# A decoder block on one core: the weight sums of a seven-product up-projection, made by vector instructions or by accumulating DMA transfers

## The chip, the core and the metric

The kernel runs on one core of a Trainium2 chip. A core has a matrix engine (TensorE, PE in the profile; its weight loads are listed apart as PEld), a vector engine (VectorE, DVE), an activation engine (ScalarE, ACT), a general engine (GpSimd, POOL), and a sync engine (SyncE, SP), which here only issues transfers. Each takes its instructions in order from its own queue, and they wait for each other by semaphores. Sixteen DMA engines move data between DRAM and the on-chip buffer. The metric is the device time of one execution in microseconds (us), the median of several runs.

## The reference

One layer, float32, 2048 tokens of width 1024:

```python
h = rms_norm(x, attn_norm_w); proj = h @ w_in
y_ret = retention_group(...)      # 8 heads, chunkwise recurrent
y_mla = mla_group(...)            # 8 heads, causal softmax attention
x = x + concat(y_ret, y_mla) @ w_out
u = rms_norm(x, ffn_norm_w) @ w_up            # (1024, 5632): gate columns, then value columns
u = conv_b + sum(conv_w[j] * pad(u)[:, j:j+S] for j in range(3))
x = x + (silu(gate) * val) @ w_down           # gate, val: the halves of u, 2816 columns each
return rms_norm(x, final_norm_w)
```

The change concerns the product with `w_up` alone.

## The kernel before

The kernel has three parts. **Input projection** (`stage_1`): norm, latents, q, k and v, written to DRAM. **Retention beside attention**: two generators, `ret_stream` and `att_stream`, are drawn from in turn (`side_by_side`); attention goes through 32 groups (8 heads by 4 groups of 512 queries, `g` = 0 to 3, group `g` with 4g + 4 blocks of keys). For a group, q and k are loaded and split into a high and a low part (`split`: ACT writes the high part, POOL the low one, lines L65 and L69), the maxima are taken (`sm`), and for each block of keys PE makes scores `s`, ACT the exponential `pc`, POOL adds `pc` to the running sum `den` (L782), and PE multiplies by v (`o`). Retention loads 1 MB tiles `h<-hT_s` through SP (L530) and multiplies them by its weights (`pm`). **The feed-forward part**, in two halves of 1024 tokens: forms of the tokens (`half_0_forms`, `half_1_forms`), the up-projection with convolution and gate (`up`), the down-projection (`down`).

Every product is three matmuls on high and low parts (`mm3`, L73 to L75). The up-projection goes through 22 blocks `fb` of 128 gate and 128 value columns. In a block, the weights are a two by two matrix of pieces, gate and value by first and second half of the 1024 rows (`g0`, `g1`, `v0`, `v1`, 128x512 each), and the tokens are split in two likewise. Seven products instead of eight make the result (a scheme of Strassen's kind): PE multiplies seven sums of weight pieces with seven sums of token pieces, and DVE adds up the results in `u` (L1136).

- `token_forms` makes the seven token sums `F` once for each half.
- `weight_forms` makes the seven weight sums of each block: the plain pieces g0, v1, g1, and v0 + v1, v0 + v1 - g0, g0 - v0, g1 + g0 - v0 - v1. The four sums are POOL instructions (L1097 one addition, L1084 three subtractions), and each of the seven is split by ACT and POOL. It is a generator that runs ahead of the products: `LEAD` (9) forms before the first, then one form a product. The twelve places for split weights are `order`.
- `up_load` loads the four pieces of a block in two DMAs of 512 KB, a block ahead, into the four buffers `raws`.
- `conv` (L1141 to L1143) and the gate (L1166 to L1168) are ACT and DVE instructions of 1024 columns.

The order on each engine is not the order of the source: a scheduler in the compiler takes the instructions of all generators and puts on each engine those that it expects to be ready, by its own costs. An engine's queue is then fixed, and an instruction whose semaphore isn't there yet holds everything behind it. SP's transfers use eight semaphores in turn, so one also waits for the eighth before it. All SP transfers go through one queue of the DMA engines, in order.

Of the kernel before, what the change touches and what calls it, by code (L numbers as in the profile page):

```python
# [11 lines left out]
F32 = mybir.dt.float32  # L12
# [3 lines left out]
ALU = mybir.AluOpType  # L16
# [4 lines left out]
P = 128  # L21
# [3 lines left out]
KC = D // P  # L25
# [4 lines left out]
NFB = DFF // P  # L30
# [24 lines left out]
class Block:  # L55
# [500 lines left out]
    def att_stream(self):  # L556

        groups = [(h, g) for h in range(H) for g in range(4)]
        qs, done = {}, set()

        def maxima():
            for n, hg in enumerate(groups):
                while n > self.at + 2:
                    yield 0
                for c, qs[n] in self.att_max(*hg):
                    yield c
                done.add(n)
        self.at, mx, owed = 0, maxima(), 0.0
        for n, (h, g) in enumerate(groups):
            self.at = n  # L570
            while n not in done:
                yield next(mx)
            for c in self.att_group(h, g, qs.pop(n)):
                owed = min(owed + MAX_PACE, 2.0)
                while owed >= 1:
                    owed -= 1
                    c += next(mx, 0)
                yield c
        self.finish()
        yield 450  # L580

    def ret_chunk(self, p, ch, W, hs):
        nc, c1, c2, px = self.nc, self.r1, self.r2, self.pr_x
# [398 lines left out]
    def half_0_forms(self):  # L982

        nc, hn = self.nc, self.fs

        def rows(i):
            for j in range(2):
                nc.sync.dma_start(hn[2 * (i % 2) + j], self.hn_s[4 * j + i])
        for t in (8, 9):
            self.z0_load(t)  # L990
        rows(0)
        rows(1)
        for i in range(4):
            self.token_forms(i, hn[2 * (i % 2)], hn[2 * (i % 2) + 1])
            if i < 2:
                rows(i + 2)
            if i == 0:
                self.up_load(0)
            for t in (8 + 2 * i, 9 + 2 * i):
                m, y = self.ms[t % 2].rearrange("p (a k x) -> p a k x", a=2, k=4), self.ys[t % 2]  # L1000
                pss = [self.bank() for _ in range(2)]
                for kc in range(4):
                    self.out_mm(pss, m, kc, kc == 0, kc == 3)
                self.out_add(y, pss)
                nc.sync.dma_start(self.y_s[t], y)
                if t + 2 < NT:
                    self.z0_load(t + 2)
        self.up_start(0)
# [20 lines left out]
    def half_1_forms(self):  # L1029

        nc, hn, fnw = self.nc, self.fs, self.u2.rearrange("p a b -> p (a b)")
        for n in range(2):
            nc.sync.dma_start(self.ys[n], self.y_s[Z1_ORDER[n]])
        self.pay()
        for n, t in enumerate(Z1_ORDER):
            m, y = self.ms[n % 2].rearrange("p (a k x) -> p a k x", a=2, k=4), self.ys[n % 2]
            pss = [self.bank() for _ in range(2)]
            for kc in range(4, 8):
                self.out_mm(pss, m, kc, kc == 4, kc == 7)
            if n + 2 < TH:  # L1040
                self.z1_load(n + 2)
            self.out_add(y, pss)
            h, ss = hn[n % 4], self.cs.tile([P, 1], F32, name="ss")
            nc.scalar.activation(h, y, AF.Square, scale=D ** -0.5, accum_out=ss)
            nc.sync.dma_start(self.y_s[t], y)
            r = self.rstd(self.cs, ss, "n")
            nc.vector.scalar_tensor_tensor(h, y, r, fnw, op0=ALU.mult, op1=ALU.mult)
            if n + 2 < TH:
                nc.sync.dma_start(self.ys[n % 2], self.y_s[Z1_ORDER[n + 2]])
            if n == 1:  # L1050
                self.up_load(0)
            if n in (3, 5):
                self.token_forms(n // 2 - 1, hn[(n - 3) % 4], hn[(n - 2) % 4])
        self.up_start(1, 1)
        self.token_forms(2, hn[0], hn[1])
        for _ in range(3):
            next(self.prep)
        self.token_forms(3, hn[2], hn[3])

    def up_load(self, fb):  # L1060
        if fb < NFB:
            for j in range(2):
                self.nc.sync.dma_start(self.raws[(2 * fb + j + 2) % 4], self.a["w_up"][j * NFB + fb].rearrange("p k f -> p (k f)"))

    def up_start(self, half, lead=None):

# [12 lines left out]

    def weight_forms(self):  # L1080

        nc, a = self.nc, self.a
        t1, t2 = (self.fs[0][:, k * 512:(k + 1) * 512] for k in range(2))
        sub = lambda o, x, y: nc.gpsimd.tensor_tensor(o, x, y, op=ALU.subtract)  # L1084
        W = self.W = {}

        def raw(fb, j, k):
            return self.raws[(2 * fb + j + 2) % 4][:, k * 512:(k + 1) * 512]

        def put(fb, n, src):  # L1090
            W[fb, n] = self.slot_split(src, P)
        for fb in range(NFB):
            self.up_load(fb + 1)
            g0, g1, v0, v1 = (raw(fb, j, k) for j in range(2) for k in range(2))
            put(fb, 0, g0)
            yield
            nc.gpsimd.tensor_tensor(t1, v0, v1, op=ALU.add)  # L1097
            sub(t2, t1, g0)
            put(fb, 1, t2)
            yield  # L1100
            sub(v0, g0, v0)
            put(fb, 6, v0)
            yield
            put(fb, 4, t1)
            yield
            sub(g0, g1, t2)
            put(fb, 2, v1)
            yield
            put(fb, 3, g0)
            yield  # L1110
            put(fb, 5, g1)
            yield

    def up(self, half):

        nc, u, F, p1 = self.nc, self.u, self.F, self.p1
        ag, av = self.fs[2], self.fs[3]  # L1120
        u2, u3 = self.u2[:, 0], self.u2[:, 1]
# [5 lines left out]
        def product(fb, n):  # L1127
            ps = self.bank()
            wh, wl = self.W.pop((fb, n))
            for kc in range(4):  # L1130
                self.mm3(ps, wh[:, kc, :], wl[:, kc, :], F[:, n, 0, kc, :], F[:, n, 1, kc, :], kc == 0, kc == 3)
            next(prep, None)
            return ps

        def add(out, ps, x):
            nc.vector.tensor_tensor(out, ps, x, op=ALU.add)  # L1136

        def conv(acc, fb, j):
            w0, w1, w2, b = (self.cw[:, j * NFB + fb, k:k + 1] for k in range(4))
            x = u[:, j]  # L1140
            nc.scalar.activation(acc, x[:, 2:1026], AF.Identity, scale=w2, bias=b)  # L1141
            nc.vector.scalar_tensor_tensor(acc, x[:, 1:1025], w1, acc, op0=ALU.mult, op1=ALU.add)  # L1142
            nc.vector.scalar_tensor_tensor(acc, x[:, 0:1024], w0, acc, op0=ALU.mult, op1=ALU.add)  # L1143
        owed = None
        if half == 0:
            nc.vector.memset(u[:, :, 0:2], 0.0)
        for fb in range(NFB):
            nc.scalar.activation(p1, product(fb, 0), AF.Copy)
            add(u2, product(fb, 1), p1)
            add(u3, product(fb, 6), u2)  # L1150
            if owed:
                nc.sync.dma_start(*owed)
            ps = product(fb, 4)
            if half:
                nc.vector.tensor_copy(u[:, :, 0:2], self.tail[:, fb])
            add(u[:, 1, 514:], ps, u3)
            add(u2, ps, u2)
            add(u[:, 1, 2:514], product(fb, 2), u3)
            conv(av, fb, 1)
            add(u[:, 0, 514:], product(fb, 3), u2)  # L1160
            add(u[:, 0, 2:514], product(fb, 5), p1)
            conv(ag, fb, 0)
# [109 lines left out]
    def run(self):  # L1272
        tc, ctx = self.tc, self.ctx
        dp = ctx.enter_context(tc.tile_pool(name="scratch", bufs=1, space=DRAM))
# [7 lines left out]
        self.rden_s = dp.tile([4, H, 4, P], F32, name="rden_s")  # L1282
        self.y_s = dp.tile([NT, P, D], F32, name="y_s")
        self.hn_s = dp.tile([TH, P, D], F32, name="hn_s")
        self.g_s = dp.tile([2, NFB, P, HALF], F32, name="g_s")
        self.den_s = dp.tile([4, H, 4, P], F32, name="den_s")
        self.denl_s = dp.tile([4, H, 4, P], F32, name="denl_s")
# [53 lines left out]
def host_arrays(x, positions, attn_norm_w, w_in, ret_gn_w, mla_q_norm_w, w_uq, mla_kv_norm_w, w_ukv,  # L1341
# [8 lines left out]
    pe = uq[:, :, 64:]  # L1350
    pe_sw = np.concatenate([pe[:, :, 16:], pe[:, :, :16]], 2)
    ukv = g(w_ukv)[0].reshape(128, H, 128)
    w_up = g(w_up)[0].reshape(KC, P, 2 * NFB, P).transpose(2, 1, 0, 3)
    conv = np.concatenate([g(conv_w)[0], g(conv_b)], 0).reshape(4, 2 * NFB, P).transpose(2, 1, 0)
    arrays = dict(
        x=c(g(x)[0]),
# [46 lines left out]
```

## Time and profile before

| | |
|---|---|
| median of 3 runs | 2937.12 us (2935.92 to 2937.17) |
| profiled execution | 2932.35 us, its span 2930.5 us |
| granted clock of TensorE, mean | 0.976 |
| PE, DVE, ACT, POOL busy | 93%, 67%, 46%, 67% of the span |
| HBM read, written | 237.64 MB, 92.75 MB |

A row of the trace gives a start and a length in us from the span's start. In the groups of instructions a mean is in ns. An engine's idle time is put down to the engine that released it. A matmul row's length includes its way through the engine, so rows that follow each other overlap; the distance of starts (0.23 us for 512 columns) is the engine's pace.

### The profile page before, as it was taken

Reading aid. Unit: us, or ns where it says so; the run is one execution under the profiler, and the core shown is the slowest. Engines: PE = TensorE matmul, PEld = TensorE weight load, DVE = VectorE, ACT = ScalarE, POOL = GpSimd, SP = SyncE. Lnnn points to the kernel's source line nnn. Section 1 sums busy time; section 2 is a strip of 40 time slices with the busy share of each in tenths; the row PEclk is TensorE's granted clock in tenths of the full one; section 3 lists DMA queues with packets and bytes.
Section 4 is the critical chain, followed back from the end, with each engine's and each line's share of the span. In section 5 each row is a group of like instructions: output and inputs, shape, how many; then the busy total and the mean of one; then the engine's idle time right before and its main releaser. Section 6 shows DMA issues by size and latency. Waiting matters only on the chain.

```text
span 2930.5 us, 37500 instructions
## 1 busy us (share of the span) xinstructions
PE 2732.9 (93%) x12672; PEld 2217.2 (76%) x12672; DVE 1972.3 (67%) x3393; ACT 1347.0 (46%) x2544; POOL 1962.2 (67%) x1480
## 2 busy tenths in 40 slices
PE   7998999998999999988999999899985999999998
PEld 6976777776777777767887777688874888887887
DVE  8756776767676776744478888834276888887243
ACT  5435566666665566641433333334334443333343
POOL 2035566666656565653799999675658999995554
PEclk9999999999999999989999999999997999999999
DMA  7663121223212121346622221365562222224463
GB/s 258 226 207 91 45 77 61 69 68 97 67 56 66 44 66 59 94 116 203 233 79 72 80 86 67 101 232 169 165 204 69 87 74 78 87 72 170 144 198 107
DMA packets 153505, 332.85 MB, mean 114 GB/s; under 512 B 35032, under 2 KB 68568, under 8 KB 147168
## 3 DMA queue, kind: packets, MB, share of 16 engines
q1 hardware_dynamic: 153312, 330.45, 34.8%
q8 instruction: 100, 1.64, 0.2%
q14 instruction: 93, 0.76, 0.1%
HBM read 237.64 MB, written 92.75 MB: 113 GB/s over the span
## 4 chain that ended last, share of the span: by engine, by line
PE 42%; DVE 10%; issue 5%; ACT 3%; POOL 2%; DMA 2%; SPq 0%; ACTq 0%; DVEq 0%; POOLq 0%
PE b L75 12%; PE b L74 12%; PE b L73 12%; DVE w L1142 2%; ACT w L1141 2%; DVE u L1136 2%; DVE w L1143 1%; DVE w L1168 1%; DMA raw<-mixa_s 1%; DVE w L1167 1%; PE x L666 1%; ACT u L1166 1%; POOL w L69 1%; PE pm L75 1%; PE pm L74 1%
## 5 line engine op out<-in xcount | busy, mean ns | idle before, releaser
L69 POOL TENSOR_TENSOR w<-raw,w 128x512 fp32r<-128x512 f32 (+2 forms) x315 | 523.5, 1677 | 251.1 <-ACT w L65 239.3
L73 PE MATMUL b<-F,w 128*128 128x512 f32 x1232 | 488.8, 397 | 3.9 <-DVE u L1136 3.9
L75 PE MATMUL b<-F,w 128*128 128x512 f32 x1232 | 491.9, 399 | 0.0
L74 PE MATMUL b<-F,w 128*128 128x512 f32 x1232 | 487.5, 396 | 3.1 <-POOL F L69 3.1
L782 POOL TENSOR_TENSOR den<-den,pc 128x512 f32<-128x512 f32 (+2 forms) x256 | 294.5, 1150 | 231.4 <-ACT pc L771 212.8
L65 ACT ACTIVATE w<-raw 128x512 fp32r<-128x512 f32 (+2 forms) x328 | 214.4, 658 | 340.5 <-PE b L75 166.3
L73 PE MATMUL b<-w 128*128 128x512 f32 x832 | 329.9, 396 | 22.0 <-DVE u L1136 13.1
L75 PE MATMUL b<-w 128*128 128x512 f32 x832 | 328.2, 394 | 1.4 <-POOL w L69 1.2
L74 PE MATMUL b<-w 128*128 128x512 f32 x832 | 327.6, 394 | 0.0
L69 DVE TENSOR_TENSOR w<-xr,w 128x512 fp32r<-128x512 f32 x88 | 108.6, 1234 | 286.3 <-ACT w L65 286.3
L73 PEld LDWEIGHTS b<-F,w 128*128 128x128 f32 x1232 | 232.6, 189 | 65.8 <-DVE u L1136 11.1
L74 PEld LDWEIGHTS b<-F,w 128*128 128x128 f32 x1232 | 232.5, 189 | 61.8 <-POOL F L69 3.6
L75 PEld LDWEIGHTS b<-F,w 128*128 128x128 f32 x1232 | 232.5, 189 | 55.0
L1141 ACT ACTIVATE w<-u,cw 128x1024 f32<-128x1024 f32 x88 | 109.5, 1244 | 332.7 <-DVE u L1136 187.1
L773 DVE TENSOR_TENSOR pc<-s,pc 128x512 fp32r<-128x512 f32 (+1 forms) x320 | 197.3, 618 | 94.8 <-ACT s L772 78.1
L771 ACT ACTIVATE pc<-s 128x512 fp32r<-128x512 f32 (+1 forms) x320 | 173.0, 540 | 177.9 <-PE s L769 173.5
L1142 DVE SCALAR_TENSOR_TENSOR w<-u,cw,w 128x1024 f32<-128x1024 f32 x88 | 165.8, 1884 | 129.2 <-ACT w L1141 129.2
L73 PE MATMUL pm<-w,h 128*128 128x512 f32 x512 | 209.1, 408 | 12.2 <-DVE r_g L115 3.8
L69 POOL TENSOR_TENSOR w<-xr,w 128x512 fp32r<-128x512 f32 x110 | 205.5, 1881 | 9.4 <-ACT w L65 9.4
L74 PE MATMUL pm<-w,h 128*128 128x512 f32 x512 | 203.9, 398 | 0.0
L73 PEld LDWEIGHTS b<-w 128*128 128x128 f32 x832 | 158.6, 191 | 59.4 <-DVE u L1136 16.8
L75 PE MATMUL pm<-w,h 128*128 128x512 f32 x512 | 203.1, 397 | 0.0
(264 smaller groups left out, 6622.3 us busy)
## 6 DMA issues: line engine op xcount, KB each, us to landing
raw<-in_w_down SPq DMA_DIRECT2D x88, 512.0 KB
h<-hT_s SPq DMA_DIRECT2D x32, 1024.0 KB
xr<-in_w_up SPq DMA_DIRECT2D x44, 512.0 KB
raw<-in_w_up SPq DMA_DIRECT2D x44, 512.0 KB
g_s<-w SPq DMA_DIRECT2D x44, 512.0 KB
xr<-g_s SPq DMA_DIRECT2D x88, 256.0 KB
hT_s<-hT SPq DMA_DIRECT2D x16, 1024.0 KB
raw<-in_w_ret SPq DMA_DIRECT2D x16, 512.0 KB
```

Of the source, the lines that this page charges most:

```text
L65: nc.scalar.activation(hi, src, AF.Copy)
L69: eng.tensor_tensor(lo, src, f32(hi), op=ALU.subtract)
L73: mm(out, lhsT=lh, rhs=rh, start=start, stop=False)
L74: mm(out, lhsT=lh, rhs=rl, start=False, stop=False)
L75: mm(out, lhsT=ll, rhs=rh, start=False, stop=stop)
L666: mm(ps[:, x * P:x * P + 256], lhsT=l, rhs=r, start=n == 0, stop=n == len(ops) - 1)
L771: nc.scalar.activation(pc[:, 0, r0:], ps[:, r0:], AF.Exp, scale=ATT_SCALE)
L773: nc.vector.tensor_tensor(pc[:, 1, r0:], ps[:, r0:], f32(pc[:, 0, r0:]), op=ALU.subtract)
L782: nc.gpsimd.tensor_tensor(den[:, r0:], den[:, r0:], hi[:, r0:], op=ALU.add)
L1136: nc.vector.tensor_tensor(out, ps, x, op=ALU.add)
L1141: nc.scalar.activation(acc, x[:, 2:1026], AF.Identity, scale=w2, bias=b)
L1142: nc.vector.scalar_tensor_tensor(acc, x[:, 1:1025], w1, acc, op0=ALU.mult, op1=ALU.add)
```

## The change

The host lays out `w_up` so that g0, g1, v0 and v1 are four arrays of [22, 128, 512]. A new generator `sums`, drawn from once at the start of each attention group, makes four sums in DRAM (`sum_s`, 4 x 22 x 128 x 512 float32): s1 = v0 + v1, s2 = v0 + v1 + g0, s3 = v0 + g0, s4 = v0 + v1 + g0 + g1. Each is a copy from DRAM to DRAM issued by SP and one accumulating transfer issued by POOL (`accum_op=ALU.add`) that adds a second array to it. It does so for blocks 0 to 10 and then for 11 to 21: eight copies and eight accumulating transfers, each of 11 x 128 x 512 x 4 bytes = 2.88 MB. The gate pieces thereby have the opposite sign in s2 to s4; `up` turns two additions into subtractions the other way round, and one more in the gate's result. `weight_forms` has no additions left: it splits each of the seven pieces as it comes from DRAM, with a load of 256 KB for each of them (`form_load`), eight forms ahead, in half buffers of `raws`.

```diff
-        self.at, mx, owed = 0, maxima(), 0.0
+        self.at, mx, owed, sums = 0, maxima(), 0.0, self.sums()
         for n, (h, g) in enumerate(groups):
             self.at = n
+            next(sums, None)
...
+    def sums(self):
+        sy, po = self.nc.sync.dma_start, self.nc.gpsimd.dma_start
+        rows = lambda t: t.rearrange("b p f -> (b p f)").rearrange("(n x) -> n x", x=2048)
+        for part in range(2):
+            sl = slice(part * NFB // 2, (part + 1) * NFB // 2)
+            g0, g1, v0, v1 = (rows(self.a["w_up"][i][sl]) for i in range(4))
+            s1, s2, s3, s4 = (rows(self.sum_s[i][sl]) for i in range(4))
+            def more(t, x):
+                po(t, x, accum_op=ALU.add, max_dma_last_dim=2048)
+            yield sy(s1, v0)
+            yield sy(s3, v0)
+            yield more(s1, v1)
+            yield more(s3, g0)
+            yield sy(s2, s1)
+            yield
+            yield more(s2, g0)
+            yield
+            yield sy(s4, s2)
+            yield
+            yield more(s4, g1)
+            yield
...
+    def form_load(self, i):
+        if i < 7 * NFB:
+            fb, n = divmod(i, 7)
+            src = [self.a["w_up"][0], self.sum_s[1], self.sum_s[2], self.sum_s[0], self.a["w_up"][3], self.sum_s[3], self.a["w_up"][1]][n]
+            self.nc.sync.dma_start(self.form_raw(i), src[fb])
+    def form_raw(self, i):
+        return self.raws[(i // 2 + 2) % 4][:, (i % 2) * 512:(i % 2 + 1) * 512]
...
     def weight_forms(self):
-        for fb in range(NFB):
-            self.up_load(fb + 1)
-            g0, g1, v0, v1 = (raw(fb, j, k) for j in range(2) for k in range(2))
-            put(fb, 0, g0)
-            yield
-            nc.gpsimd.tensor_tensor(t1, v0, v1, op=ALU.add)
-            sub(t2, t1, g0)
-            put(fb, 1, t2)
-            yield
-            sub(v0, g0, v0)
-            put(fb, 6, v0)
...
-            sub(g0, g1, t2)
...
+        for i in range(4, 8):
+            self.form_load(i)
+        for i in range(7 * NFB):
+            fb, n = divmod(i, 7)
+            W[fb, (0, 1, 6, 4, 2, 3, 5)[n]] = self.slot_split(self.form_raw(i), P)
+            self.form_load(i + 8)
             yield
...
-            add(u2, product(fb, 1), p1)
-            add(u3, product(fb, 6), u2)
+            sub(u2, product(fb, 1), p1)
+            sub(u3, u2, product(fb, 6))
...
-            add(u[:, 0, 514:], product(fb, 3), u2)
+            sub(u[:, 0, 514:], product(fb, 3), u2)
```

Of SP's queue before, at the start of attention (q, k and v of the first group, and the next tiles `h` of retention):

```order
L462 DMA mqk<-in_mask_att 128x128 [waits DMAHW1_49,DVE_49,Pool_49]
L723 DMA raw<-q_s 96x512 [waits DMAHW2_49,Activation_49]
L530 DMA h<-hT_s 128x2048 [waits DMAHW3_49,PE_49]
L707 DMA raw<-k_s 64x512 [waits DMAHW4_49,DMAHW0_49,Activation_49]
L708 DMA raw<-kpe_s 34x512 [waits DMAHW5_49]
L710 DMA raw<-v_s 128x4x64 [waits DMAHW6_49]
L723 DMA raw<-q_s 96x512 [waits DMAHW7_49,DMAHW2_49,Pool_49]
L530 DMA h<-hT_s 128x2048 [waits PE_49]
```

The same place of SP's queue now (`sum_s` is the DRAM array of the sums):

```order
L462 DMA mqk<-in_mask_att 128x128 [waits DMAHW1_49,DVE_49,Pool_49]
L594 DMA sum_s<-in_w_up 64x11264 [waits DMAHW2_49]
L748 DMA raw<-q_s 96x512 [waits DMAHW3_49,Activation_49]
L732 DMA raw<-k_s 64x512 [waits DMAHW4_49,DMAHW0_49,Activation_49]
L733 DMA raw<-kpe_s 34x512 [waits DMAHW5_49]
L735 DMA raw<-v_s 128x4x64 [waits DMAHW6_49]
L595 DMA sum_s<-in_w_up 64x11264 [waits DMAHW7_49]
L748 DMA raw<-q_s 96x512 [waits DMAHW3_49,Pool_49]
L732 DMA raw<-k_s 64x512 [waits DMAHW5_49,DMAHW4_49,DMAHW6_49,DMAHW1_49,Pool_49]
L733 DMA raw<-kpe_s 34x512 [waits DMAHW2_49]
L735 DMA raw<-v_s 128x4x64
L530 DMA h<-hT_s 128x2048 [waits PE_49]
```

Two copies, and the loads of two groups, now stand ahead of the first tile `h`, which stood right behind the first load of q.

SP's queue now, 38 rows after the first copy: the last four of the eight copies (DMASW is a semaphore of an accumulating transfer).

```order
L602 DMA sum_s<-sum_s 64x11264 [waits DMAHW0_49,DMASW2_49]
L821 DMA den_s<-otl 1x512 [waits DMAHW1_49,Activation_49]
L595 DMA sum_s<-in_w_up 64x11264 [waits DMAHW2_49]
L748 DMA raw<-q_s 96x512 [waits DMAHW6_49,DMAHW5_49,DMAHW7_49,DMAHW3_49,Pool_49]
L598 DMA sum_s<-sum_s 64x11264 [waits DMAHW4_49,DMASW3_49]
L602 DMA sum_s<-sum_s 64x11264 [waits DMASW6_49]
L724 DMA mix_s<-m 128x2x128 [waits Activation_49]
L530 DMA h<-hT_s 128x2048 [waits PE_49]
L732 DMA raw<-k_s 64x512 [waits DMAHW0_49,Pool_49]
```

All sixteen transfers have been put into the first three attention groups, not one into each of 24 groups; three of these copies wait for accumulating transfers, the last for the seventh of the eight.

POOL's queue now, at the end of the third attention group (`den`: the running sum of the softmax; `pc`, `ot`: the group's end):

```order
L593 DMA sum_s<-in_w_up 1408x512 [waits DMAHW4_49]
L807 TENSOR_TENSOR den<-den,pc 128x512 [waits Activation_49,Pool_49] x2
L641 TENSOR_TENSOR vs<-vg,gam 128x128 [waits Activation_49]
L807 TENSOR_TENSOR den<-den,pc 128x384 [waits Activation_49,Pool_49]
L807 TENSOR_TENSOR den<-den,pc 128x256 [waits Activation_49,Pool_49]
L593 DMA sum_s<-in_w_up 1408x512 [waits DMAHW5_49]
L807 TENSOR_TENSOR den<-den,pc 128x256 [waits Activation_49,Pool_49]
L69 TENSOR_TENSOR q<-raw,q 96x512 [waits PE_49,Activation_49]
L69 TENSOR_TENSOR pc<-den,pc 128x512 [waits DVE_49,Activation_49]
L845 TENSOR_TENSOR ot<-ot,otl 64x512 [waits Activation_49]
```

These are the seventh and the eighth accumulating transfer; the eighth waits for the last copy, and the group's last addition to `den` stands behind it.

## Rows read from the trace of the kernel before

**Rows 1.** The page: span, and each engine's busy time and share

```profile
span 2930.5 us, 37500 instructions
PE 2732.9 (93%) x12672; PEld 2217.2 (76%) x12672; DVE 1972.3 (67%) x3393; ACT 1347.0 (46%) x2544; POOL 1962.2 (67%) x1480
```

**Rows 2.** Stretches: length, busy us of each engine, clock, DMA share, GB/s

```profile
core 0: us, PE busy (x) PEld busy (x) DVE busy (x) ACT busy (x) POOL busy (x), PEclk, DMA share, GB/s
221.50:299.50 78.00, 64.98 (x308) 49.40 (x307) 52.02 (x122) 43.70 (x95) 46.36 (x46) 0.93 0.29 85
1388.00:1455.00 67.00, 59.51 (x287) 50.42 (x288) 34.08 (x59) 27.24 (x48) 41.87 (x34) 0.95 0.73 249
1560.00:1860.00 300.00, 296.10 (x1254) 233.85 (x1253) 248.13 (x210) 114.52 (x165) 287.64 (x165) 1.00 0.22 78
2160.00:2250.00 90.00, 50.72 (x206) 39.23 (x205) 70.84 (x123) 34.91 (x64) 70.25 (x53) 0.77 0.41 137
2250.00:2650.00 400.00, 400.00 (x1712) 321.77 (x1711) 334.55 (x277) 157.62 (x219) 386.09 (x217) 1.00 0.22 77
```

**Rows 3.** Groups of POOL in 1560 to 1860: busy us, mean ns

```profile
L69 POOL TENSOR_TENSOR w<-xr,w 128x512 fp32r<-128x512 f32 x38 | 76.0, 2007 | 4.7 <-ACT w L65 4.7
L1097 POOL TENSOR_TENSOR w<-raw 128x512 f32<-128x512 f32 x8 | 17.2, 2156 | 0.6
L1084 POOL TENSOR_TENSOR raw<-raw,w 128x512 f32<-128x512 f32 x8 | 10.4, 1299 | 0.6
```

**Rows 4.** Groups of DVE in 1560 to 1860

```profile
L1142 DVE SCALAR_TENSOR_TENSOR w<-u,cw,w 128x1024 f32<-128x1024 f32 x30 | 58.9, 1964 | 40.4 <-ACT w L1141 40.4
L1168 DVE SCALAR_TENSOR_TENSOR w<-w 128x1024 f32<-128x1024 f32 x15 | 33.1, 2207 | 0.5
```

**Rows 5.** The chain that ended last, in order of time, late in half 0

```profile
1887.57 1.29 DVE w L1142
```

**Rows 6.** PE in order of time, 1600 to 1681: with the wait before

```profile
1614.82 0.50 PE L73 MATMUL b<-F,w 128*128 128x512 f32 x1 [0.28 <-DVE u L1136]
1634.95 0.50 PE L73 MATMUL b<-F,w 128*128 128x512 f32 x1 [0.27 <-DVE u L1136]
```

**Rows 7.** The chain, 2205 to 2250: ten pieces of L1084 and L1097

```profile
2210.82 1.27 POOL w L1084
...
2242.51 0.43 POOL xr L1084
```

**Rows 8.** SP's issues in order of time, start of attention and the next `h`

```profile
221.44 0.39 SPq L462 DMA_DIRECT2D mqk<-in_mask_att  x1
221.93 0.37 SPq L723 DMA_DIRECT2D raw<-q_s  x1
222.40 0.38 SPq L530 DMA_DIRECT2D h<-hT_s  x1
...
299.52 0.34 SPq L530 DMA_DIRECT2D h<-hT_s  x1
```

**Rows 9.** POOL in order of time: the end of the third attention group

```profile
309.37 0.73 POOL L782 TENSOR_TENSOR den<-den,pc 128x256 f32<-128x256 f32 x1 [3.06 <-PE x L666]
310.11 1.29 POOL L69 TENSOR_TENSOR q<-raw,q 96x512 fp32r<-96x512 f32 x1
311.37 1.29 POOL L69 TENSOR_TENSOR pc<-den,pc 128x512 fp32r<-128x512 f32 x1
```

More of the change, by code (lines that the diff above doesn't have):

```diff
@@ L997, in half_0_forms @@
             if i == 0:
-                self.up_load(0)
+                self.forms_begin()
             for t in (8 + 2 * i, 9 + 2 * i):
@@ L1050, in half_1_forms @@
             if n == 1:
-                self.up_load(0)
+                self.forms_begin()
             if n in (3, 5):
@@ L1058, in half_1_forms, with forms_begin @@
         self.token_forms(3, hn[2], hn[3])
[L1060 to L1063, printed above, removed]
+    def form_load(self, i):
[5 more added lines that the diff above has]
+        return self.raws[(i // 2 + 2) % 4][:, (i % 2) * 512:(i % 2 + 1) * 512]
+    def forms_begin(self):
+        for i in range(4):
+            self.form_load(i)
     def up_start(self, half, lead=None):
@@ L1080, in weight_forms @@
     def weight_forms(self):
-        nc, a = self.nc, self.a
-        t1, t2 = (self.fs[0][:, k * 512:(k + 1) * 512] for k in range(2))
-        sub = lambda o, x, y: nc.gpsimd.tensor_tensor(o, x, y, op=ALU.subtract)
         W = self.W = {}
[L1087 to L1091, printed above, removed]
-        for fb in range(NFB):
-            self.up_load(fb + 1)
-            g0, g1, v0, v1 = (raw(fb, j, k) for j in range(2) for k in range(2))
-            put(fb, 0, g0)
-            yield
-            nc.gpsimd.tensor_tensor(t1, v0, v1, op=ALU.add)
-            sub(t2, t1, g0)
-            put(fb, 1, t2)
-            yield
-            sub(v0, g0, v0)
-            put(fb, 6, v0)
-            yield
-            put(fb, 4, t1)
-            yield
-            sub(g0, g1, t2)
[L1107 to L1111, printed above, removed]
+        for i in range(4, 8):
+            self.form_load(i)
+        for i in range(7 * NFB):
+            fb, n = divmod(i, 7)
+            W[fb, (0, 1, 6, 4, 2, 3, 5)[n]] = self.slot_split(self.form_raw(i), P)
+            self.form_load(i + 8)
             yield
@@ L1136, in add, with sub @@
             nc.vector.tensor_tensor(out, ps, x, op=ALU.add)
+        def sub(out, x, y):
+            nc.vector.tensor_tensor(out, x, y, op=ALU.subtract)
         def conv(acc, fb, j):
@@ L1284, in run @@
         self.hn_s = dp.tile([TH, P, D], F32, name="hn_s")
+        self.sum_s = dp.tile([4, NFB, P, 512], F32, name="sum_s")
         self.g_s = dp.tile([2, NFB, P, HALF], F32, name="g_s")
@@ L1352, in host_arrays @@
     ukv = g(w_ukv)[0].reshape(128, H, 128)
-    w_up = g(w_up)[0].reshape(KC, P, 2 * NFB, P).transpose(2, 1, 0, 3)
+    w_up = g(w_up)[0].reshape(2, 4, P, 2, NFB, P).transpose(3, 0, 4, 2, 1, 5).reshape(4, NFB, P, 512)
     conv = np.concatenate([g(conv_w)[0], g(conv_b)], 0).reshape(4, 2 * NFB, P).transpose(2, 1, 0)
```

## The prediction, as written before the run

> **What bounds the kernel now.** I read the page first, then the stretches, then one order of time for each place that the change touches.
>
> The page says that PE is busy 93% of a span of 2930.5 us, DVE and POOL 67% each [rows 1]. That is an average over stages with different limits, so what POOL's relief is worth has to be read where POOL works hardest. The stretches show two such places. In the up-projection POOL is busy 287.6 of 300 us in the first half and 386.1 of 400 in the second, but PE is busy 296.1 and 400.0 there [rows 2]: POOL is nearly full, and PE is what sets the pace. The forms ahead of the second half are the exception: PE is busy only 50.7 of 90 us, POOL 70.3 [rows 2], and there the chain of waits runs through POOL's additions [rows 7].
>
> The place where the change adds work looks different. At the start of attention, from 221.5 to 299.5, PE is busy 65 of 78 us, POOL 46, and the DMA engines are busy 29% [rows 2]. That reads as room for transfers. Whether it is depends on what stands behind them in the queues, which the order of the queues shows.
>
> **What the change removes.** Each block has one addition of 2.16 us and three subtractions of 1.30 us on POOL [rows 3], 6.1 us in all, of the 20 us that a block takes. Their worth in the two places:
>
> - First half, steady state. 1254 matmuls take 300 us, 0.2392 us each; in the second half 1712 take 400 us, 0.2336 each [rows 2]. A block has 7 x 12 = 84 matmuls, so 22 blocks lose 22 x 84 x 0.0056 = 10.3 us in the first half to a wait at the end of a block: 0.28 us shown as a wait for DVE's `u`, and a slow start behind it [rows 6]. DVE is late because its instructions with two operands stretch beside POOL: L1142 takes 1.96 us in the mean and L1168 2.21 [rows 4], while an L1142 late in this half, with POOL's load down, took 1.29 [rows 5]. With 4 of 11 POOL instructions of a block gone I expect the wait to go, and PE to be late next: 10 us. The second half has nothing to give; what POOL saves there is idle time.
> - Forms ahead of the second half. Ten of the chain's pieces are L1084 and L1097; the lengths add to 11.2 us, from 1.27 at 2210.8 to 0.43 at 2242.5 [rows 7]. The splits of the same forms stay, and each form now waits for a load of its own; I take 10 of the 11.2. Ahead of the first half PE is busy 59.5 of 67 us [rows 2], and I count nothing.
>
> Together a gain of 20 us, at most 22, at least 0. The three subtractions in place of additions on DVE have the same operands and size, and cost nothing. The smaller loads, seven of 256 KB in place of four pieces in two DMAs, add 0.79 MB a block to engines busy 22% [rows 2]; a form is loaded eight forms, some 22 us, ahead, so PE covers them.
>
> **What the change adds.** Eight copies and eight accumulating transfers of 2.88 MB. Their number in 24 groups would be one in some 30 us, but the order of the queues puts all of them into the first three groups, and makes a chain of them. Follow it from the end. POOL's last addition to `den` in the third group now stands behind the eighth accumulating transfer. That one waits for the eighth copy. The eighth copy, in SP's queue, waits for the seventh accumulating transfer, and the retention tile `h` and the next k stand behind it. And copies and loads of SP go through one queue in order. So POOL can't come to this `den` before eight copies and seven accumulating transfers have landed. Before, that took from the first load of q at 221.93, where the first copy now stands [rows 8], to 309.37 [rows 9]: 87.4 us. The `h` behind the copies was issued at 299.52 [rows 8] and says the same. Behind `den` wait the softmax tiles that PE needs next; PE can't go far.
>
> Now the chain's length. No row shows a transfer from DRAM to DRAM or an accumulating one, so both are bounded.
>
> - A copy. The sixteen engines, at 73% busy, moved 249 GB/s [rows 2], 341 GB/s if full. At that rate 2.88 MB takes 8.5 us. Every byte here is in DRAM at both ends; if reading and writing took turns, 16.9 us. I take the middle, 12.7, since no row is nearer to one of them.
> - An accumulating transfer is in pieces of 2 KB, as the order shows (1408 x 512), much like the loads of attention. These ran at 85 GB/s at 29% [rows 2], 293 GB/s if full: 9.8 us for each passage of 2.88 MB. It reads two arrays and writes one. The low end is one passage at the better rate, 8.5; the high end three passages, 29.5. I take two, 19.7: the two reads after each other, the write beside them.
> - The kernel's own transfers in the 78 us are 0.29 x 78 = 22.6 us of the engines [rows 2].
>
> Sum: 8 x 12.7 + 7 x 19.7 + 22.6 = 262 us in place of 87.4, a delay of 175 us. What hides it? PE has work for the three groups, and that is the 87.4 already taken off. The low end, with the kernel's own transfers beside the others, is 8 x 8.5 + 7 x 8.5 = 127.5, a delay of 40. The high end, 8 x 16.9 + 7 x 29.5 + 22.6 = 364, is a delay of 277.
>
> For the copy, the Trainium skill, DMA: Bandwidth & Descriptors, section Latency and other measured facts, has 214 GB/s for a copy between two tensors in HBM at full rate. By that an estimate of a copy is 13.5 us, and the sum would be 6 us longer; no run here has shown one yet.
>
> Net: 175 - 20 = 155 us on the profiled 2932.35, 3087. The median of the runs is 4.8 us above that execution, so 3092 for the median. With the low delay and the full gain 2932 + 40 - 22 + 5 = 2955; with the high delay and no gain 3214.
>
> **Rivals.**
>
> 1. *The transfers hide, and the gain stays.* The chain fits into the first groups, and the result is 2937 - 20 = 2917. For it: engines busy 29% and PE with work. Against it: fifteen transfers would have to be done in 87.4 - 22.6 + 20 = 85 us to break even, 5.7 us or 508 GB/s each, where 341 is what full engines moved with one end on the chip.
> 2. *An accumulating transfer costs two copies.* If its two reads take turns at the copy's own pace of 12.7, it takes 25.4 us and the delay is 8 x 12.7 + 7 x 25.4 + 22.6 - 87.4 = 215: 3132. For it: its two operands both lie in DRAM. Against: nothing in the rows has a second read. The Trainium skill, Collectives: The Full Stack, section on the bandwidth ceiling, states this rule: a reducing transfer moves at half a plain one's rate, since it needs two reads. The trace of before has no such transfer to check it.
> 3. *POOL's descriptors set the pace.* POOL, not SP's hardware, writes the descriptors of 1408 pieces. From 19.7 us / 1408 = 14 ns a piece on, that decides. At 24 ns a transfer takes 33.8 us, the delay is 8 x 12.7 + 7 x 33.8 + 22.6 - 87.4 = 273, and the time 3190. SP issues a load of 96 rows in 0.37 us [rows 8], about 4 ns a row, which speaks against it, but that is another engine.
>
> **How the numbers follow.** The forecast, slower by 2955 to 3190 with 3092 the likeliest: 0.60. Rival 2, 0.17; rival 3, 0.10; both are slower too. Rival 1, 0.10, since a queue's order that I read wrongly would be enough for it. Delay and gain alike by chance: 0.03. A difference within 0.2% (5.9 us) is what a measurement of this kernel can't tell from none. So slower 0.87, same 0.03, faster 0.10. The range of 8 in 10 leaves out rival 1, the equal case and the top of rival 3: 2960 to 3205. It is wide because a copy and an accumulating transfer are unknown within factors of two and three.
>
> **What would show it.** Right: a hole in PE between about 225 and 480, with k, q, `h` and POOL's `den` as what is waited for; the DMA engines near full there; the sixteen transfers issued within the first three groups; a copy at 10 to 17 us and an accumulating one at 15 to 30 from issue to the next waiter; after that, attention as before. In `up`, no wait for `u` at the ends of blocks in the first half and 10 us less; POOL idle a third of the time there; some 10 us less ahead of the second half. Wrong: if PE's work in attention takes as long as before, the chain's reading is wrong, and rival 1 holds. If the delay is right but POOL shows long spans at the transfers, rival 3. If `up` is not shorter, the wait for `u` is DVE's own.

## The result, and the profile after

The changed kernel takes 3005.3 us in the median (3002.9 to 3011.0); the kernel before took 2935.9 in runs between them. The ratio is 1.0245, with a 95% interval of 1.0231 to 1.0259: slower by some 72 us. The forecast was slower by 155.

The page of the changed kernel, span and engines, answers to [rows 1]:

```profile
span 3008.1 us, 37863 instructions
PE 2741.4 (91%) x12672; PEld 2227.2 (74%) x12672; DVE 1868.7 (62%) x3393; ACT 1372.2 (46%) x2544; POOL 1596.2 (53%) x1312
```

POOL lost 366 us of work and DVE 104, and yet the span grew by 77.6. Where, the starts of the products of the up-projection tell (PE's rows `b<-F,w`, in us; "between" is the first down-projection and the forms of the second half):

| | first product | first up | between | second up | second down |
|---|---|---|---|---|---|
| before | 1447.9 | 439.2 | 350.9 | 439.0 | 253.5 |
| changed | 1563.4 | 431.0 | 332.9 | 432.7 | 248.1 |
| difference | +115.5 | -8.2 | -18.0 | -6.3 | -5.4 |

So 115.5 us are lost before the up-projection and 38 won from there on. The stretches of the changed kernel (columns as in [rows 2]; the last three are the first up, the 90 us ahead of the second, and the second up) show both:

```profile
221.50:299.50 78.00, 51.28 (x200) 38.22 (x201) 34.11 (x98) 29.37 (x64) 32.74 (x33) 0.78 1.00 273
299.50:425.00 125.50, 50.34 (x194) 38.41 (x192) 24.98 (x54) 21.28 (x44) 30.27 (x29) 0.67 1.00 235
...
1670.00:1970.00 300.00, 300.00 (x1287) 241.36 (x1286) 222.26 (x216) 126.97 (x168) 161.97 (x107) 1.00 0.40 122
2249.00:2339.00 90.00, 60.51 (x246) 47.01 (x246) 73.67 (x139) 38.06 (x69) 59.44 (x44) 0.79 0.53 173
2350.00:2750.00 400.00, 400.00 (x1716) 321.77 (x1715) 300.94 (x289) 171.26 (x226) 210.31 (x141) 1.00 0.40 119
```

At the start of attention the DMA engines went from 29% to full, PE from 65 busy us in 78 to 51, and then to 50 in 125; its granted clock fell to 0.67 in the mean, so part of the time it ran at the lower of its two levels. In the first up PE makes 1287 matmuls in 300 us where it made 1254, and POOL is at 54% instead of 96%. POOL and DVE in the first up, which answer to [rows 3, 4]:

```profile
L69 POOL TENSOR_TENSOR w<-xr,w 128x512 fp32r<-128x512 f32 x54 | 81.3, 1510 | 72.7 <-ACT w L65 72.7
L1157 DVE SCALAR_TENSOR_TENSOR w<-u,cw,w 128x1024 f32<-128x1024 f32 x30 | 38.5, 1284 | 40.2 <-ACT w L1156 40.2
L1183 DVE SCALAR_TENSOR_TENSOR w<-w 128x1024 f32<-128x1024 f32 x16 | 35.3, 2209 | 0.5
```

The first of the two convolution steps is down from 1.96 us to 1.28, the length that one late in the half had before [rows 5]; the gate's step at 2.21 is as it was. PE waits for nothing in this stretch (0.28 us at the end of a block before [rows 6]).

The chain, in order of time of the changed kernel, SP's copies (L594, L598, L602) and POOL's accumulating transfers (L593):

```profile
222.84 0.57 SPq L594 DMA_DIRECT2D sum_s<-in_w_up  x1
234.84 1.62 POOL L593 DMA_DIRECT2D sum_s<-in_w_up  x1
...
294.30 0.53 SPq L594 DMA_DIRECT2D sum_s<-in_w_up  x1
307.11 1.50 POOL L593 DMA_DIRECT2D sum_s<-in_w_up  x1 [0.37 <-DMA sum_s<-in_w_up]
...
359.39 0.47 SPq L598 DMA_DIRECT2D sum_s<-sum_s  x1
374.73 1.48 POOL L593 DMA_DIRECT2D sum_s<-in_w_up  x1 [20.93 <-DMA sum_s<-sum_s]
412.63 0.47 SPq L602 DMA_DIRECT2D sum_s<-sum_s  x1
424.34 1.50 POOL L593 DMA_DIRECT2D sum_s<-in_w_up  x1 [43.38 <-DMA sum_s<-sum_s]
425.25 1.35 POOL L807 TENSOR_TENSOR den<-den,pc 128x256 f32<-128x256 f32 x1
```

The last row is the `den` that stood at 309.37 [rows 9]: 115.9 us later, and the first product of the up-projection is 115.5 later. It does stand behind the eighth accumulating transfer, which waits for the eighth copy, which waits for the seventh accumulating transfer. Who waits, from 222 to 460 (engine, tile, line, us in total, times, longest):

```profile
POOL sum_s L593 <- DMA sum_s<-sum_s: 74.8, 4, 43.4
...
PE sm L770 <- DVE n L69: 43.8, 3, 41.2
...
ACT k L65 <- DMA raw<-kpe_s: 21.1, 4, 15.0
```

How long POOL takes to issue an accumulating transfer (ns, least, median, most) and how long one takes to land:

```profile
L593 POOL DMA_DIRECT2D sum_s<-in_w_up x8: 1477/1496/1622, 234.8 to 424.3; - x8
...
DMA to landing us min/median/max: 20.7/39.1/52.3
```

1.5 us for 1408 pieces is 1.06 ns a piece, far from the 14 at which rival 3 begins. But a landing takes 39 us in the median, twice what the prediction took, and yet the sum was too long. The experiments were made to say why.

### The profile page after: what moved, and what is told of

The parts are those of the page before. It is cut to its first block, busy times and chain, and to the rows that moved or that the text cites. A ratio compares the mean times of both kernels' runs of the same rounds, so it can differ in the third digit from the quotient of the medians.

```text
span 3008.1 us, 37863 instructions
## 1 busy us (share of the span) xinstructions
PE 2741.4 (91%) x12672; PEld 2227.2 (74%) x12672; DVE 1868.7 (62%) x3393; ACT 1372.2 (46%) x2544; POOL 1596.2 (53%) x1312
## 4 chain that ended last, share of the span: by engine, by line
PE 53%; DVE 3%; DMA 2%; POOL 2%; issue 1%; ACT 1%; SPq 0%; POOLq 0%; ACTq 0%; DVEq 0%
PE b L75 15%; PE b L73 15%; PE b L74 15%; DMA raw<-mixa_s 1%; PE x L691 1%; PE u L75 1%; PE pm L75 1%; PE pm L74 1%; PE pm L73 1%; PE u L74 1%; PE u L73 1%; DMA p<-rden_s 0%; PE sm L757 0%; POOL raw L882 0%; DMA w<-y_s 0%
## 5 line engine op out<-in xcount | busy, mean ns | idle before, releaser
L69 POOL TENSOR_TENSOR w<-raw,w 128x512 fp32r<-128x512 f32 (+2 forms) x357 | 538.6, 1522 | 414.7 <-ACT w L65 398.4
L65 ACT ACTIVATE w<-raw 128x512 fp32r<-128x512 f32 (+2 forms) x370 | 242.8, 659 | 514.9 <-PE b L74 195.1
L69 POOL TENSOR_TENSOR w<-xr,w 128x512 fp32r<-128x512 f32 x156 | 233.9, 1506 | 191.6 <-ACT w L65 191.6
L65 ACT ACTIVATE w<-xr 128x512 fp32r<-128x512 f32 x244 | 151.9, 625 | 182.8 <-PE b L74 153.5
L761 DVE TENSOR_REDUCE mx<-sm 128x1 f32<-128x512 f32 x192 | 131.7, 686 | 89.1 <-PE sm L757 87.9
```

Of the source, the lines that this page charges most:

```text
L65: nc.scalar.activation(hi, src, AF.Copy)
L69: eng.tensor_tensor(lo, src, f32(hi), op=ALU.subtract)
L761: nc.vector.tensor_reduce(mx[:, i, c:c + 1], ps[:, :w], axis=AX, op=ALU.max)
```

## The experiments

In the groups below each run's time is the median, with the ratio to the kernel before and its 95% interval.

**Loss and gain apart.** e1 keeps `weight_forms` and `up` of before and adds the transfers; e2 and e3 are the changed kernel without all transfers, or without the accumulating ones.

```diff
 e2: -            next(sums, None)
     -            src = [..., self.sum_s[1], self.sum_s[2], ...][n]
     +            src = self.a["w_up"][(0, 1, 2, 2, 3, 0, 1)[n]]
 e3: -                po(t, x, accum_op=ALU.add, max_dma_last_dim=2048)
     +                pass
```

> The sixteen transfers are made as in the changed kernel, but nothing reads their sums: the up-projection keeps its POOL additions and subtractions. Theory A (the transfers cost about 115 us at the start of attention, as POOL's last den of the third group moved from 309.4 to 425.3, and the rest of the kernel gains about 38): 2936 + 115 = 3051, 3043 to 3059. Rival G (the gain is the predicted 20, the rest of the drift is something else, so the transfers cost only 90 in the end): 3026. The prediction's own chain (175): 3111.

> The sixteen transfers are left out, and the loads of the sums read plain pieces of the weights in their place (this leaves the four weight sums out of the result); everything else is as in the changed kernel. Theory A: only the gain remains, 2936 - 38 = 2898, 2893 to 2903. Rival G (gain 20 as predicted): 2916.

> The eight accumulating transfers are left out, the eight copies stay (so the sums are plain copies of v0). Theory A, terms additive: 8 x 12.5 + 22.6 = 123 in place of 87.4 us, a delay of 35, and the gain of 38: 2933. If copies alone hide beside work, since nothing waits for them except by SP's queue: 2898 to 2910. Rival B (the cost is traffic, wherever it falls: copies move 46 of 115 MB read or written): 2936 + 115 x 0.4 - 38 = 2944.

e1: 3042.0 us, 1.0374 (1.0353 to 1.0396). e2: 2898.4, 0.9882 (0.9867 to 0.9897). e3: 2908.2, 0.9920 (0.9901 to 0.9938). The loss by e1 is 109 us, the gain by e2 34.5, and their difference, 74.5, is the changed kernel's 72 within the intervals. The gain of 20 is too small (rival G falls). Copies alone cost 10 us over e2, not the 35 of waits laid end to end. The 115.5 of the table is not all due to the transfers: the first product of e1 comes 107.0 us later than before, and that of e2, which has no transfer, 5.6 later, for a reason that no run shows. So e2's stages win 38 too, and its time 34.5.

**One strict chain.** e5 makes each copy read what the transfer before it wrote.

```diff
-            yield sy(s1, v0)
-            yield sy(s3, v0)
-            yield more(s1, v1)
-            yield more(s3, g0)
-            yield sy(s2, s1)
...
+            yield sy(s1, v0 if part == 0 else last)
+            yield more(s1, v1)
+            yield sy(s3, s1)
+            yield more(s3, g0)
+            yield sy(s2, s3)
...
+            last = s4
```

> The sixteen transfers of the changed kernel are made one strictly after the other: each copy reads what the accumulating transfer before it wrote (so the sums are of other pieces), eight links of copy and accumulate in all, still in the first three groups. Alone, a copy was seen to take about 12.2 us (e3) and an accumulating transfer 20.0 to 20.6 (e4), close to the 12.7 and 19.7 of the prediction. Theory A (the terms were right, and what failed was that they follow each other: in the changed kernel two chains ran beside each other): 8 x 12.2 + 7 x 20.3 = 240 us from the first copy to POOL's den, at most 22.6 more, in place of 87.4; a delay of 153 to 175, and the time 2898 + 153 to 175 = 3051 to 3073. Rival D (the bytes set it, not the order): as the changed kernel, 3005.

3014.0 us, 1.0263 (1.0240 to 1.0286). The time is that of rival D, but the trace says that both expectations missed something. Order of time and landing in e5:

```profile
223.07 0.57 SPq L594 DMA_DIRECT2D sum_s<-in_w_up  x1
...
426.38 1.51 POOL L593 DMA_DIRECT2D sum_s<-in_w_up  x1 [20.93 <-DMA sum_s<-sum_s]
...
445.77 0.50 SPq L600 DMA_DIRECT2D sum_s<-sum_s  x1
457.31 1.48 POOL L593 DMA_DIRECT2D sum_s<-in_w_up  x1 [19.51 <-DMA sum_s<-sum_s]
458.21 1.86 POOL L804 TENSOR_TENSOR den<-den,pc 128x512 f32<-128x512 f32 x1
...
DMA to landing us min/median/max: 18.0/19.0/22.7
```

The chain of eight copies and seven accumulating transfers takes 234.2 us, close to the 239.5 of the prediction's own terms (8 x 12.7 + 7 x 19.7). But the scheduler put the eighth transfer behind more of POOL's own work this time. The `den` behind it stood here in the kernel before:

```profile
337.49 1.31 POOL L782 TENSOR_TENSOR den<-den,pc 128x512 f32<-128x512 f32 x1
```

So it is late by 120.7, not by 153 to 175: my expectation had taken the place in POOL's queue as fixed. In series, then, the terms of the prediction for the transfers hold, and the kernel's own 22.6 us, which its sum added, run beside them. In the changed kernel the two parts of the sums were two chains beside each other, and from 222.8 to 424.3 the engines were full (DMA share 1.01, next to last column):

```profile
222.80:424.30 201.50, 100.89 (x391) 76.07 (x390) 57.78 (x147) 50.64 (x108) 61.96 (x59) 0.71 1.01 250
```

and the page gives the accumulating queue's work (packets, MB, share of 16 engines):

```profile
q0 software_dynamic: 11392, 23.07, 4.3%
```

4.3% of 3008 us in eight transfers is 16.2 us of the engines each. The packets of the 201.5 us, added up by queue and size, say the same and give the rest: 114.1 us of the engines for the seven accumulating transfers (16.3 each), 63.1 for the eight copies (their packets have 45,056 bytes; 7.9 each) and 25.4 for the kernel's own. Together they are 202.6, as long as the stretch: the engines' work fills it, and the waits overlap. In e5 the work of a transfer is nearly the same (8.3 and 16.3), the chain is single, and it takes 33 us longer at a DMA share of 0.91.

**Spread over the groups.** e4 holds each transfer, from the second on, behind the end of the attention group before it; e10 asks for its copies in pieces of 2 KB; e6 and e9 issue the copies from POOL's queue, e6 as they were and e9 in pieces. In the traces e10's copies have packets of 2,048 bytes and e9's of 4,096, in place of 45,056.

```diff
+                with self.tc.issue_after(self.tail_sp), self.tc.issue_after(self.tail_po):
                     next(sums, None)
 e6: +        sy = self.nc.gpsimd.dma_start
 e9: +        sy = lambda t, x: self.nc.gpsimd.dma_start(t, x, max_dma_last_dim=2048)
 e10: +       sy = lambda t, x: self.nc.sync.dma_start(t, x, max_dma_last_dim=2048)
```

> The sixteen transfers are held in the order of the queues behind the end of one attention group each (SP's and POOL's own last instruction of the group before), so that they lie over 24 groups; all else as in the changed kernel. Theory A (the cost is the chain in three groups, and in the queues that the kernel's own work stands behind): with a group between a transfer and the next that needs it, the cost falls to 0 to 10 us, and the time is 2898 to 2908, faster than the kernel before. Rival B (traffic costs the same wherever it falls): 3005. Between: each copy delays the loads of SP by 12 us, 8 x 5 = 40 us of it shown: 2938.

> As e4 (copies from SP's queue), with the copies cut into 2 KB pieces. Theory K with one queue in order: loads issued behind a copy still stand behind all of it, so little comes back: 2925 to 2940. If the piece alone matters: 2900 to 2915.

> As e4 (one transfer behind the end of each attention group), and the eight copies too are issued by POOL, into its queue of the DMA engines, so that no load of SP stands behind a copy in one queue. Theory Q (what e4 still lost, 41 us over e2, is SP's loads of k and their like standing 12 us behind a copy, and PE at half clock after such a wait): nearly all comes back, 2898 to 2910. Rival B (it is the engines' bandwidth, shared with the transfers): 2930 to 2940. POOL's own time for eight more issues is 8 x 1.5 = 12 us, hidden.

> As e6 (transfers spread over the groups, all from POOL's queue), but a copy is cut into 1408 pieces of 2 KB, as the accumulating transfers are, in place of 64 of 45 KB. In e6 a load of k beside a copy landed about 14 us after its neighbours' usual 3, although in another queue, and the copy's packets took 2.16 us each. Theory K (an engine takes the queues' packets in turn, so a small load waits one 45 KB packet for each of its own): with 2 KB packets the loads pass, and the time falls from 2969 to 2898 to 2915. Rival B (bandwidth): 2960 or more.

e4: 2939.1, 1.0019 (1.0010 to 1.0028). e10: 2941.4, 1.0026 (1.0017 to 1.0036). e6: 2968.8, 1.0118 (1.0096 to 1.0139). e9: 2964.2, 1.0102 (1.0085 to 1.0119). Spreading takes back 66 of the 107 us by which the changed kernel stands over e2, so the chain in three groups was most of the loss; but 41 us stay in e4, the value named between the two theories. An accumulating transfer with no other beside it now lands about as the prediction had it (19.7):

```profile
DMA to landing us min/median/max: 20.0/20.5/23.6
```

What stays is seen at a copy at the change to a new head (e4, SP's issues, then ACT):

```profile
517.06 0.56 SPq L607 DMA_DIRECT2D sum_s<-sum_s  x1
...
518.20 0.35 SPq L530 DMA_DIRECT2D h<-hT_s  x1
518.61 0.27 SPq L738 DMA_DIRECT2D raw<-kpe_s  x1
...
533.23 0.63 ACT L65 ACTIVATE k<-raw 98x512 fp32r<-98x512 f32 x1 [4.33 <-DMA raw<-kpe_s]
```

The load of `kpe_s` is behind the copy and used 14.6 us after its issue; the same load is used 5.4 us after its issue in e2. PE has little to do meanwhile, and then its granted clock is at the lower of its two levels (columns as in [rows 2]):

```profile
528.00:533.00 5.00, 2.06 (x10) 1.48 (x10) 2.68 (x9) 0.90 (x2) 1.26 (x1) 0.94 0.95 283
533.00:538.00 5.00, 2.74 (x7) 1.77 (x6) 3.06 (x6) 3.75 (x9) 3.54 (x4) 0.50 0.05 15
```

I took the late load for the order of one queue (theory Q). It isn't that alone: with the copies in another queue, e6, ACT waits longer for these loads, and smaller pieces (theory K; 4 KB in the trace) change little (e9: 46.0). ACT's waits for them in the same part of attention, in e2, e4 and e6:

```profile
ACT k L65 <- DMA raw<-kpe_s: 13.1, 10, 2.6
```

```profile
ACT k L65 <- DMA raw<-kpe_s: 26.8, 12, 4.3
```

```profile
ACT k L65 <- DMA raw<-kpe_s: 46.6, 10, 9.6
```

Both theories fell: in these runs a small load beside a 2.88 MB copy is late whatever its queue. In which way the engines share is open. Nor are these waits the whole of the 41 us: e4's are 13.7 us longer than e2's. PE's largest wait there is for ACT's `otl`, 22.9 us in e4 and 5.2 in e2 (where its wait for DVE's `mx` is longer, 13.8 in place of 6.9):

```profile
PE sm L762 <- ACT otl L825: 22.9, 13, 5.8
```

That e6 is 30 us worse than e4 is in part a matter of place. With nothing to hold it, its first copy went out at the very start of the kernel, and the first load of q came at 231.3 us in place of 221.6:

```profile
1.67 0.70 POOL L599 DMA_DIRECT2D sum_s<-in_w_up  x1
```

The rest of the difference is seen (the longer waits at POOL's copies) but not explained.

**Other places and sizes.** e11 is e4 with transfers only at the start of the two long groups of a head; e12 adds POOL's queue and the pieces (4 KB in the trace). e14 makes the sums in eleven parts of two blocks, 88 transfers, each behind one of POOL's `den`.

```diff
 e11: +            if g >= 2:
                       with self.tc.issue_after(self.tail_sp), self.tc.issue_after(self.tail_po):
                           next(sums, None)
 e14: +                if self.turn % 5 in (0, 2, 4) or self.turn > 250:
      +                    with self.tc.issue_after(ins.ins):
      +                        next(self.sum_it, None)
```

> As e4, with the same coarse copies on SP, but a transfer only at the start of the two long groups of a head (g = 2 and 3, some 40 and 50 us each), so none falls on the change to a new head, where k, v and q are loaded anew. If what e4 lost is lost at these changes: 2898 to 2912. If a copy costs its 2 to 5 us wherever it lies: 2930 to 2940.

> Both: transfers only in the long groups, all from POOL's queue, all in 2 KB pieces. Theory K and the places: 2898 to 2908, faster than both kernels. Rival B (bandwidth): 2930 or more.

> All else as in the changed kernel; the sums are made in eleven parts of two blocks in place of two parts of eleven (88 transfers of 0.52 MB), all from POOL's queue, each held behind one of POOL's additions to den, three of them to five additions, and a link of a part's chain at least two transfers behind the one before it. Theory S (what is left of the cost in e11, 23 us, is a burst of 12 to 20 us in which the loads crawl; a burst of 3 to 4 us is covered by their lead): 2900 to 2912, faster than every kernel so far with all sums. Rival T (the bytes cost the same however they are cut, as 2 KB pieces in e9 showed): 2930 to 2965. POOL's time: 88 issues of some 0.6 us are 53 us, of which POOL has 38% free.

e11: 2921.8, 0.9956 (0.9941 to 0.9971). e12: 2923.3, 0.9964 (0.9952 to 0.9976). e14: 2925.1, 0.9963 (0.9949 to 0.9977). Three versions with all sums made by transfers beat the kernel before by 10 to 12 us. All missed their expectations, by 10 to 15 us: neither the place nor the length of a burst removes the last 23 to 27 us over e2, though they take away 34 to 43% of e4's. e11 and e12 agree within their intervals, so in the long groups queue and pieces make no difference that these runs can tell; and all these kernels move the same bytes as e9, which rival B (bandwidth) had right, so the bytes alone don't set the cost. In e11 ACT's wait is nearly back:

```profile
ACT k L65 <- DMA raw<-kpe_s: 17.8, 13, 5.6
```

**Where the gain is from.** e8 has no transfers; POOL makes the sums in the first half as before, SP stores them, and the second half loads them. e7, e13 and e15 are e2 with four POOL instructions a block in the two ups that nobody reads: reading the loads (e7), reading idle buffers (e13), and these held between the splits (e15).

```diff
 e8:  +        def keep(k, src):
      +            nc.sync.dma_start(self.sum_s[k, fb], src)
 e13: +            for _ in range((0, 2, 1, 0, 0, 1, 0)[n] if i >= LEAD else 0):
      +                self.nc.gpsimd.tensor_tensor(self.fs[0][:, 0:512], self.fs[0][:, 512:], self.fs[1][:, 0:512], op=ALU.subtract)
 e15: +                with self.tc.issue_after(self.last_split.ins):
```

> No transfers in attention. In the first half POOL makes the sums as before, and SP stores the four of each block to DRAM (1 MB a block); the second half loads them, as the changed kernel does. The first half's gain of 8 is lost, the gain between and in the second half stays. Theory A: 18 + 6 + 5 = 29 at most, 2933 - 20 to 29 = 2904 to 2913, faster than both kernels. If part of the 18 belongs to the end of the first half: 2915 to 2920. If the stores hold up POOL: 2930 or more.

> As e2 (no transfers, no sums), with POOL given back four additions of 128x512 a block in the two up-projections, which nobody reads; the nine forms ahead of each up-projection have none. Theory P (POOL's load in the up-projections is what costs time there, and through DVE's late u also at the start of the down-projection; it is 8 of the first half, 6 of the second, and part of the 18 between): 2898 + 14 to 25 = 2912 to 2923. Rival L (what costs is that a form waits for a sum before it is split; a POOL instruction that nobody reads costs nothing): 2898 to 2901.

> As e7 (no transfers, no sums; four POOL subtractions of 128x512 a block that nobody reads, in the up-projections only), but they read and write buffers that no load and no split uses there, so that they wait for nothing; in e7 they waited for loads, and SP's store g_s stood behind these. Theory P (POOL's load in the up-projections costs by itself, through DVE's longer instructions and late u): 2898 + 8 + 6, with a part of the 18 between the two: 2912 to 2923. Rival L (only the wait of a split for its sum costs): 2898 to 2903. Rival W (what e7 lost was POOL's load after all, not its waits): 2980 to 2990.

> As e13 (no transfers, no sums; four POOL subtractions of 128x512 a block that nobody reads, in the up-projections only), but each is held behind the split before it in POOL's queue; in e13 they ran in two clumps at the start of the up-projections (56 of them between 1470 and 1600). Theory P (POOL's load costs by itself): the first up-projection goes back from 431 to 439, the start of the down-projections loses 10 to 18, the second up 6: 2898 + 14 to 32 = 2912 to 2930. Rival L (only the wait of a split for its sum costs): 2898 to 2903.

e8: 2917.4, 0.9948 (0.9930 to 0.9965), the lowest median of the kernels with all sums, though its interval and e11's overlap; it is the value named for the case that part of the 18 belongs to the end of the first half. e7: 2992.1, 1.0194 (1.0172 to 1.0216), and e13: 3045.1, 1.0372 (1.0357 to 1.0388), lie outside every value expected for POOL's load and tell nothing of it: each was upset by its own placing. In e7 (1600 to 1800) the added instructions wait for loads, and SP's store `g_s` comes so late that ACT waits for it; in e13 they ran in clumps, 56 of them between 1470 and 1600:

```profile
ACT w L1157 <- DMA g_s<-w: 67.9, 9, 8.1
```

```profile
L1121 POOL TENSOR_TENSOR w<-w 128x512 f32<-128x512 f32 x56 | 80.0, 1428 | 2.9
```

e15: 2910.8, 0.9933 (0.9916 to 0.9949), 12 us over e2 and just below the 2912 of theory P; the stages tell which of its terms hold. The same table for the three that can be read:

| | first up | between | second up | second down |
|---|---|---|---|---|
| e2 | 431.0 | 333.1 | 432.3 | 248.1 |
| e8 | 439.1 | 348.5 | 433.1 | 247.9 |
| e15 | 431.0 | 345.1 | 433.4 | 249.4 |

The first up and a group of DVE in e15:

```profile
1560.00:1860.00 300.00, 300.00 (x1288) 241.34 (x1287) 248.38 (x211) 115.15 (x165) 289.97 (x166) 1.00 0.39 118
...
L1159 DVE SCALAR_TENSOR_TENSOR w<-u,cw,w 128x1024 f32<-128x1024 f32 x30 | 57.8, 1926 | 40.2 <-ACT w L1158 40.2
```

POOL is as full as before (290 of 300 us), DVE's step as long (1.93 us), and the first up still takes 431.0, with PE never waiting. So its 8 us are not POOL's load. The start of the first down-projection, though, loses its gain in e15. PE's waits for `u` in the first 26 us of it, before, in e15 and in e8 (in e2 there are none):

```profile
PE b L73 <- DVE u L1136: 10.1, 4, 5.3
```

```profile
PE b L73 <- DVE u L1153: 5.6, 2, 4.6
PE b L73 <- DVE u L1150: 2.4, 1, 2.4
```

```profile
PE b L73 <- DVE u L1165: 10.2, 4, 4.7
```

## Why the prediction was right in direction and wrong in size

- *Bounds and queue.* Right: the transfers land in the first three groups, POOL's `den` stands behind the last of them, and PE has its hole there. The delay of 115.9 at this `den` is still 115.5 at the first product. Rival 1 (it hides) falls; even spread, the transfers show 23 us or more.
- *The chain's length: the step that failed.* The sum 8 x 12.7 + 7 x 19.7 + 22.6 = 262 added waits in series; measured, 201.5. Its prices for a transfer are right for one after the other (e5: 234.2 against 239.5, with the kernel's own transfers beside them), and an accumulating transfer with no other beside it lands in 20.5 (19.7 taken). What failed is that they follow each other: two chains ran beside each other (the second part's first copy goes out at 294.30, the first part's last at 325.26), and then the engines' work counts, 7.9 for a copy in place of 12.7 and 16.3 for an accumulating transfer in place of 19.7. That takes 38 and 24 us off, the kernel's own transfers put 3 on, and 262 becomes 203. The lower bound of the copy, 8.5, from the rate of full engines, was near the right price for a transfer that shares them. The delay is 116 in place of 175.
- *The rules cited.* By the Trainium skill, DMA: Bandwidth & Descriptors, section Latency and other measured facts, a copy takes an estimated 13.5 us; in e5 one took 10.7 to 13.2 from its issue to the transfer that waits for it, 11.4 in the median, so it is a little faster. By the Trainium skill, Collectives: The Full Stack, section on the bandwidth ceiling, a reducing transfer (there the step of a ring) moves at half a plain one's rate. The trace agrees for the engines' work (16.3 against 7.9); in time alone it is 19.0 against 11.4, a factor of 1.7. Rival 2 priced the wait with it, 25.4 us, and was too high.
- *Rival 3* falls by POOL's 1.5 us for an issue; its price of 24 ns a piece stood on no row.
- *The gain's two places.* The first up gave 8.2 (10 taken). The forms ahead of the second half gave 5.3 up to the first product and 6.3 in the first block of the second up, which took 27.4 us before and 21.1 now; there PE waited 3.1 us for a split of token forms by POOL, and its granted clock was 0.64 in the mean of 2238 to 2250. Together 11.6 (10 taken). The sentence that the second half's up has nothing to give was read from 2250 on [rows 2], 12 us behind its start. PE's wait in before, 2237 to 2270:

```profile
PE b L74 <- POOL F L69: 3.1, 1, 3.1
```

- *The place that was missed.* The down-projections gave 12.7 (the first one's length, 320.5 to 307.8) and 5.4. The wait of 10.1 us for `u` at the start of the first was in the trace of before. For the first it is POOL's load in the up: all of it comes back in e15, where the length is 320.9, and in e8, which loads POOL in the first half alone, it comes back too, and the second's doesn't. Of the second's 5.4 only 1.3 come back in e15; what the others are, no run shows. Places and missed place make 38, in place of 20.
- *The reason given for the first up fell.* DVE's long instructions beside POOL don't make PE late in the up itself (e15). Whether it is the split's wait for its sum, or the order of DVE's and POOL's instructions that went with it, no run separates.

The two errors have the same sign: 59 us too much lost, 18 too little won, of the 87 between 3092 and 3005; the rest, some 10, is the difference between one profiled execution and the medians.

## What to carry to other kernels

Before transfers are priced as a chain, look whether other chains run beside it: alone, a transfer costs its time to land (here e5), beside others its share of full engines (here the changed kernel). Draw a transfer's place from the order of the queues, not from the line in the source where it is issued, and hold it there by an explicit edge if the place matters. When a busy engine is relieved, look for the gain at the seams between stages, where PE waits for that engine's backlog, and not only in the steady state where PE is full.

## What was not expected of the hardware

- A load of 34 x 512 values beside a DRAM-to-DRAM copy of 2.88 MB was used some 14 us after its issue, in the copy's queue (e4) or in another (e6, e9), with the copy in packets of 45 KB (e4, e6) or of 4 KB (e9). Without the copy it was 5.4 us (e2).
- The DMA engines' share reached 1.01 over 200 us: the times of the packets add to more than the engines' time, so some of them overlap, and a share near 1 is no sum of waits. One chain alone kept it at 0.91 (e5).
- Four POOL subtractions a block more or less, with DVE's two-operand steps at 1.93 or 1.28 us, made no difference to an up-projection that PE fills (431.0 us in the first half, e15 and e2).
